# Heads in pairs, a later turning, later constant rows, and a longer lag in the feed-forward stage

## The chip, the core and the metric

The kernel runs on one core of a Trainium2 chip. A core has a matrix engine (TensorE, in the rows PE, with its loads of the stationary operand as PEld), a vector engine (VectorE, DVE), a scalar engine (ScalarE, ACT), a general engine (GpSimd, POOL) and a queue engine (SyncE, SP) that starts transfers. Each engine works through its own list of instructions in order, and waits where an instruction needs what another engine has not yet made. The metric is the device time of one execution in microseconds; less is better.

## The reference: what is computed

Two layers over 256 tokens of width 1024. In each layer a normalised input goes through one wide projection whose columns feed four mixers: A, attention over chunks with a position bias; B, attention on low-rank queries and keys with a rotary part; C, attention with forget sums in the scores; D, a convolution module. A, B and C have four heads of 64 columns each, so there are twelve heads. Each mixer's 256 columns are projected to 1024, multiplied with a sigmoid gate, and summed; an output projection and the residual follow. Then a feed-forward part (FF): `x + square(relu(norm(x) @ w_up)) @ w_down`, with 4096 hidden columns. A last normalisation closes the trunk.

```python
proj = jnp.einsum('bsnc,ncd->bsnd', branches, w_branch)
gates = jax.nn.sigmoid(h @ w_gate + b_gate).reshape(b, s, N_BRANCH, D_MODEL)
x = x + jnp.sum(gates * proj, axis=2) @ w_o
hf = rms_norm(x, g_ffn)
x = x + jnp.square(jax.nn.relu(hf @ w_up)) @ w_down
```

## The kernel before

**Products.** Every product with a weight is made of three matmuls of a reduced float32 format (fp32r): weight and activation are each split into a high part and a remainder, and high x high, high x low and low x high are summed in PSUM (`mm3`, lines 117 to 121). A weight tile (128 x 1024, 512 KB) is loaded by SyncE, its high part is cast by ScalarE (`hi`, L112), and its remainder is subtracted by VectorE (`lo`, L113). There are five buffers for raw tiles and four each for `hi` and `lo`, so a tile is cast when the tile four places ahead of it has been used. The attention itself (scores, transposes, weighted sums) uses plain float32 matmuls, each done in two recorded passes; a transpose is one record.

**Order.** TensorE's order is as written in the program. The order on the other engines is made by the framework's planner, from its own estimate of when each instruction could run.

**Ticks.** Attention is cut into small pieces that are put between the weight products. The list `side` holds 33 slots; each weight tile of a projection or gate ends with `tick()`, which runs the next slot. Slots 0 to 3 fall into the first projections of mixer A, 4 to 7 into `values`, 8 into `mla` (the low-rank projections of B), 9 to 12 into the projections of C, and the rest into `gates`. Head i (0 to 3 of A, 4 to 7 of B, 8 to 11 of C) has its `scores` in slot 4 + 2i, its `transposes` three slots later and its `weighted` sum four slots later. So an even slot holds the weighted sum of head i-2 and the scores of head i, and an odd slot one head's transposes.

**One head.** `scores` (L561) is two products, 128 x 128 and 128 x 256, into one PSUM tile. VectorE adds mask or bias and takes the row extreme (L569), ScalarE takes the exponential with its row sum (L571), VectorE the reciprocal (L573), and GpSimd multiplies (L575, two instructions). Then TensorE transposes three blocks (L581), ScalarE copies them to SBUF (L583), and TensorE makes the weighted sum (L592, L593) into 64 of the 128 rows of a PSUM tile which two heads share: an even head into rows 0 to 63, an odd one into 64 to 127. Mixer A's scores use 64 contraction rows, 0 to 63 for an even head and 64 to 127 for an odd one; those of B and C use all 128. Score tiles come from a pool with one buffer (`psc`), the transposes' from one with two (`pms`), the weighted sums' from one with one (`ppv`).

**Constant rows.** `setup` (L214) makes, once, near the start of layer 0, the one-hot mask `hm` and, with four VectorE instructions (L219), the constant rows of mixer C's query tile `QC`. They are first read by the scores of head 8.

**Branches and output.** Gated branch sums are gathered in `Z[0]` and `Z[1]`, for the two halves of the columns. `turned(c)` transposes half c on TensorE into two PSUM tiles (L759); ScalarE and VectorE split them into `yh` (L761) and `yl` (L762). `output(kp, h)` then multiplies a weight tile of the output projection with blocks 2kp and 2kp+1 of y. Blocks 0 to 3 are half 0, blocks 4 to 7 half 1.

**Feed-forward.** There are 32 tiles. `mtile` makes the first product of tile i (24 matmuls of 256 columns), `hidden(i)` makes relu-squared and splits it (L833 to L836) into a ring of eight, and `second(d, ...)` makes the second product of tile d = i - LAG (12 matmuls of 512 columns, L853 to L857). The first three tiles (`EARLY`) are done ahead of the loop. The last two tiles of the second product (four in the last layer) are held back and done output block by output block after the loop.

Of the kernel before, what the change touches and what calls it, by code (L numbers as in the profile page):

```python
# [17 lines left out]
F32 = mybir.dt.float32  # L18
# [6 lines left out]
P = 128  # L25
# [22 lines left out]
A0 = 4  # L48
CONV_FROM, CONV_TO = 4, 28
WARM = 9  # L50

LAG = 2
RING = 8
FT = 32

# [15 lines left out]
def hybrid_trunk(ctx: ExitStack, tc: tile.TileContext, xT, xtok, pos, small, gfin, bgate, abias, w_lat, w_v, w_in, w_uq, w_ukv,  # L71
# [11 lines left out]
    psc = ctx.enter_context(tc.tile_pool(name="psc", bufs=1, space=bass.MemoryType.PSUM))  # L83
    ppv = ctx.enter_context(tc.tile_pool(name="ppv", bufs=1, space=bass.MemoryType.PSUM))
    pms = ctx.enter_context(tc.tile_pool(name="pms", bufs=2, space=bass.MemoryType.PSUM))
# [4 lines left out]
    def nm(s):  # L90
        count[0] += 1
        return f"{s}_{count[0]}"

    def after(inst, other):
        tc.add_manual_dep(inst.ins, other.ins.name,
                          mybir.DependencyInfo(mybir.DependencyClass.NoSync, mybir.DependencyReason.DATA),
                          reason="order")
# [4 lines left out]
    def weights(src, n=WCOLS, pieces=1, between=None):  # L102
        raw = rawp.tile([P, WCOLS], F32, tag="raw", name=nm("raw"))
        hi = whp.tile([P, WCOLS], F32R, tag="hi", name=nm("hi"))
        lo = wlp.tile([P, WCOLS], F32R, tag="lo", name=nm("lo"))
        w = n // pieces
        for c in range(0, n, w):
            nc.sync.dma_start(raw[:, c:c + w], src[:, c:c + w])
            if c == 0 and between is not None:
                between()  # L110
        for c in range(0, n, w):
            cut = nc.scalar.copy(hi[:, c:c + w], raw[:, c:c + w])  # L112
            done = nc.vector.tensor_tensor(lo[:, c:c + w], raw[:, c:c + w], hi[:, c:c + w], op=ALU.subtract)  # L113
        share[0] = done
        return hi, lo, done, cut
# [98 lines left out]
    def setup(prev):  # L214
        after(nc.gpsimd.tensor_copy(identr, ident), prev)
        after(nc.vector.tensor_reduce(hm, ident.rearrange("p (g c) -> p c g", c=32)[:, 0:HEADS, :], axis=AX, op=ALU.add), share[0])
        for h in range(HEADS):
            f = 64 * (1 - h % 2)
            nc.vector.tensor_scalar(QC[f:f + 32, h, :], tri[f:f + 32, P:T].unsqueeze(1).broadcast_to([32, 2, P]),  # L219
                                    hm[f:f + 32, h:h + 1], None, op0=ALU.mult)  # L220
# [75 lines left out]
    def to_features(half, dst, gcol, pool, tag):  # L296

        for pr in range(2):
            pt = pool.tile([P, 512], F32, tag=tag, name=nm("pt"))
            for j in range(2):  # L300
                k = 4 * half + 2 * pr + j
                for b in range(NB):
                    nc.tensor.transpose(pt[:, j * T + b * P:j * T + (b + 1) * P], X[:, b, k * P:(k + 1) * P], ident)  # L303
            for j in range(2):
                k = 4 * half + 2 * pr + j
                scale_split(dst, k, pt[:, j * T:(j + 1) * T], gcol(k))
# [4 lines left out]
    def ps2(ps):  # L311
        return ps.rearrange("p (a t) -> p a t", a=2)
# [12 lines left out]
    for l in range(L):  # L325
# [5 lines left out]
        side = []  # L331
# [6 lines left out]
        def new_ps(name):  # L338
            return pmm.tile([P, 512], F32, tag="mm", name=nm(name))
# [51 lines left out]
        if l == 0:  # L391
            setup(last_add)
# [143 lines left out]
        def operands(i):  # L536
            mixer, h = divmod(i, HEADS)
            pr, o = h // 2, 64 * (h % 2)
            if mixer == 1:
                return mixer, h, qB[:, h, :], kB[:, h, :], VB, h * HD  # L540
            if mixer == 2:
                return mixer, h, QC[:, h, :], KC[:, h, :], VAC, 256 + h * HD
            return mixer, h, qkA[o:o + 64, pr, :], qkA[o:o + 64, 2 + pr, :], VAC, h * HD
# [10 lines left out]

        def scores(i):
            mixer, h, q, k, _, _ = operands(i)
            S = psc.tile([P, 512], F32, tag="sc", name=nm("S"))
            for b in range(NB):
                sl = S[:, spans[b][0]:spans[b][1]]
                n = (b + 1) * P  # L560
                nc.tensor.matmul(sl, q[:, b * P:(b + 1) * P], k[:, 0:n], start=True, stop=True)  # L561
            mask = (abt[h], maskb, maskc)[mixer]
            mn = tmp.tile([P, NB], F32, tag="mn", name=nm("mn"))
            sme = tmp.tile([P, NB], F32, tag="sme", name=nm("sme"))
            pe = probs[i] = tmp.tile([P, 3 * P], F32, tag="pe", name=nm("pe"))
            for b, (c0, c1) in enumerate(spans):

                bias = mask[:, T - (c1 - c0):T]
                nc.vector.tensor_tensor_reduce(out=pe[:, c0:c1], in0=S[:, c0:c1], in1=bias, scale=-1.0, scalar=-NEG,  # L569
                                               op0=ALU.add, op1=ALU.min, accum_out=mn[:, b:b + 1])  # L570
                last_exp[0] = nc.scalar.activation(pe[:, c0:c1], pe[:, c0:c1], AF.Exp, bias=mn[:, b:b + 1], scale=-1.0,  # L571
                                                   accum_out=sme[:, b:b + 1])
            nc.vector.reciprocal(sme, sme)  # L573
            for b, (c0, c1) in enumerate(spans):
                nc.gpsimd.tensor_scalar(pe[:, c0:c1], pe[:, c0:c1], sme[:, b:b + 1], None, op0=ALU.mult)  # L575
# [95 lines left out]
            tick()  # L671


        NH = 3 * HEADS
        NT = max(A0 + 2 * NH + 3, CONV_TO + 5)
        plan = [[] for _ in range(NT)]
        for i in range(NH):
            plan[A0 + 2 * i].append((2, scores, i))
            plan[A0 + 2 * i + 3].append((1, transposes, i))
            plan[A0 + 2 * i + 4].append((0, weighted, i))  # L680
        side = [[(lambda f=f, i=i: f(i)) for _, f, i in sorted(p, key=lambda e: e[0])] for p in plan]
        side[0].append(position_biases)
        side[0].append(lambda: latents(share[0]))
# [6 lines left out]
        side[4].append(rotary_key_rows)  # L690
        if l == 0:
            side[5].append(rotary_tables)
        side[13].append(forget_sums)
        for t in range(CONV_FROM, CONV_TO):
            n = [2 * CONV_K * (j - CONV_FROM) // (CONV_TO - CONV_FROM) for j in (t, t + 1)]
# [11 lines left out]
        def tokens(ps, st, w, j, first, last):  # L707

            mm3(ps, st, (w[0][:, j * 512:(j + 1) * 512], w[1][:, j * 512:(j + 1) * 512]), first, last, late_mov=True)

        def block(pair, k, b):
            return pair[0][:, k, b * P:(b + 1) * P], pair[1][:, k, b * P:(b + 1) * P]
# [36 lines left out]
        def turned(c):  # L749

            if c == 0:
                y[:] = [act.tile([P, 8, T], F32R, tag="qk1", name=nm("yh")),
                        act.tile([P, 8, T], F32R, tag="qk2", name=nm("yl"))]
            for pr in range(2):
                pt = pms.tile([P, 512], F32, tag="ms", name=nm("pyt"))
                for j in range(2):
                    o = (2 * pr + j) * P
                    for b in range(NB):
                        nc.tensor.transpose(pt[:, j * T + b * P:j * T + (b + 1) * P], Z[c][:, 0, b, o:o + P], ident)  # L759
                ks = slice(4 * c + 2 * pr, 4 * c + 2 * pr + 2)  # L760
                nc.scalar.copy(y[0][:, ks, :], ps2(pt))  # L761
                nc.vector.tensor_tensor(y[1][:, ks, :], ps2(pt), y[0][:, ks, :], op=ALU.subtract)  # L762
# [26 lines left out]
        def joined(b, h):  # L789

            xs = X[:, b, h * 512:(h + 1) * 512]
            nc.vector.tensor_tensor(xs, po[b, h], xs, op=ALU.add)

        def output(kp, h):
            w = weights(w_o[l, kp, h])
            for b in range(NB):
                if kp == 0:
                    po[b, h] = new_ps("po")
                for j in range(2):
                    k = 2 * kp + j  # L800
                    tokens(po[b, h], block(y, k, b), w, j, k == 0, k == KT - 1)
                if kp == 3:
                    joined(b, h)
                    if (h, b) == (1, 0):
                        to_features(0, xg2, gffn, pms, "ms")
# [8 lines left out]
        branch(1, 3)  # L814
        output(0, 1)
        output(1, 0)
        output(1, 1)
        turned(1)
        for kp, h in ((2, 0), (2, 1), (3, 0), (3, 1)):
            output(kp, h)  # L820
        v2 = stream_squares()
# [41 lines left out]
        last = []  # L863
        for i in range(FT + LAG):
            if EARLY <= i < FT:
                ps = new_pu(i)
                mtile(ps[:, :T], w_up[l, i], xg2)
                hidden(i, ps)
            d = i - LAG
            if d < 0:  # L870
# [130 lines left out]
```

## Time and profile before

| what | value |
|---|---|
| time, median of 3 runs | 839.18 us (838.95 to 839.31) |
| time of the profiled execution | 839.31 us |
| its span, first to last instruction | 837.5 us |
| TensorE busy | 818.6 us, 98% |
| VectorE busy | 571.2 us, 68% |
| ScalarE busy | 438.7 us, 52% |
| GpSimd busy | 94.1 us, 11% |
| mean granted TensorE clock | 0.997 |

In a row of the timeline the first number is the start, the second how long the merged instructions lasted; matmuls are pipelined, so they overlap, and the distance between two starts is the time that one takes up. A note in brackets is idle time of the engine ahead of the row, and what ended it. In a row of the waits stand the total, the number of times, and the longest.

### The profile page before, as it was taken

The page shows a single profiled execution, that of the slowest core. Times are in us where ns is not written, and L with a number is a line of the kernel's source. Part 1 is how long each engine was busy: PE and PEld are TensorE (multiplying, and loading weights), DVE is VectorE, ACT ScalarE, POOL GpSimd, SP SyncE. Part 2 cuts the span into 40 slices and gives each one's busy share as a digit, 9 for nine tenths or more (in the row PEclk, how much of TensorE's full clock was granted, in tenths as well). Part 3 has the DMA queues.
Part 4 walks back from the last instruction along what each step waited for, and adds up shares of the span by engine and source line. Part 5 has one row for each costly group of instructions (what it writes and reads, how often), then busy time and mean ns, then how long its engine had stood idle before and what let it go on. Part 6 is the DMA issues. An engine that isn't in the chain of part 4 may idle for free. (4 is left out here: it accounts for less than half of the span.)

```text
span 837.5 us, 12579 instructions
## 1 busy us (share of the span) xinstructions
PE 818.6 (98%) x4718; PEld 708.5 (85%) x4718; DVE 571.2 (68%) x934; ACT 438.7 (52%) x703; POOL 94.1 (11%) x136
## 2 busy tenths in 40 slices
PE   9899999999999999999999999999999999999996
PEld 7888777888789999999899887778887899999994
DVE  7789875689675555555588788658795655555554
ACT  6665656444364444454485664565445544444443
POOL 6212321011100000000000222211120000000000
PEclk9999999999999999999999999999999999999998
DMA  8675545676546666656555545546655666655641
GB/s 273 226 220 165 143 151 165 185 215 200 176 138 191 187 189 190 188 182 196 168 173 177 157 126 170 166 144 200 205 185 176 186 190 183 190 186 186 188 127 51
DMA packets 44973, 148.93 MB, mean 178 GB/s; under 512 B 5488, under 2 KB 7792, under 8 KB 44784
## 3 DMA queue, kind: packets, MB, share of 16 engines
q1 hardware_dynamic: 44336, 146.51, 56.9%
q10 hardware_dynamic: 576, 1.62, 0.6%
q8 instruction: 37, 0.61, 0.3%
q14 instruction: 24, 0.20, 0.1%
HBM read 147.06 MB, written 1.05 MB: 177 GB/s over the span
## 5 line engine op out<-in xcount | busy, mean ns | idle before, releaser
L113 DVE TENSOR_TENSOR lo<-raw,hi 128x1024 fp32r<-128x1024 f32 (+2 forms) x273 | 341.1, 1253 | 199.6 <-ACT hi L112 195.7
L112 ACT CAST hi<-raw 128x1024 fp32r<-128x1024 f32 (+2 forms) x273 | 279.2, 1025 | 338.5 <-issue 213.0
L119 PE MATMUL pu<-xgh,hi 128*128 128x256 f32 x512 | 144.9, 283 | 0.7 <-ACT xgh L293 0.7
L120 PE MATMUL pu<-xgl,hi 128*128 128x256 f32 x512 | 145.1, 283 | 0.3
L121 PE MATMUL pu<-xgh,lo 128*128 128x256 f32 x512 | 144.9, 283 | 0.0
L119 PE MATMUL pgt<-hi,xgh 128*128 128x512 f32 x256 | 105.8, 413 | 0.0
L119 PE MATMUL pd<-hi,u 128*128 128x512 f32 x256 | 100.8, 394 | 1.7 <-ACT u L835 1.7
L120 PE MATMUL pd<-hi,u 128*128 128x512 f32 x256 | 100.7, 393 | 1.0 <-DVE u L836 1.0
L119 PEld LDWEIGHTS pu<-xgh,hi 128*128 128x128 f32 x512 | 98.0, 191 | 3.4 <-ACT xgh L293 1.1
L120 PEld LDWEIGHTS pu<-xgl,hi 128*128 128x128 f32 x512 | 98.0, 191 | 3.0 <-DVE xgl L294 0.7
L121 PE MATMUL pgt<-lo,xgh 128*128 128x512 f32 x256 | 100.1, 391 | 0.0
L120 PE MATMUL pgt<-hi,xgl 128*128 128x512 f32 x256 | 99.9, 390 | 0.0
L121 PE MATMUL pd<-lo,u 128*128 128x512 f32 x256 | 99.6, 389 | 0.0
L121 PEld LDWEIGHTS pu<-xgh,lo 128*128 128x128 f32 x512 | 98.0, 191 | 0.0
L575 POOL TENSOR_SCALAR pe<-pe,sme 128x128 f32<-128x128 f32 (+1 forms) x48 | 45.6, 960 | 171.4 <-DVE sme L573 161.3
L119 PEld LDWEIGHTS pd<-hi,u 128*128 128x128 f32 x256 | 48.3, 189 | 11.0 <-ACT u L835 2.5
L121 PEld LDWEIGHTS pgt<-lo,xgh 128*128 128x128 f32 x256 | 48.1, 188 | 10.8
L121 PEld LDWEIGHTS pd<-lo,u 128*128 128x128 f32 x256 | 48.1, 188 | 10.3
L119 PEld LDWEIGHTS pgt<-hi,xgh 128*128 128x128 f32 x256 | 48.1, 188 | 9.8 <-issue 0.7
L120 PEld LDWEIGHTS pd<-hi,u 128*128 128x128 f32 x256 | 48.3, 189 | 9.5 <-DVE u L836 1.8
L120 PEld LDWEIGHTS pgt<-hi,xgl 128*128 128x128 f32 x256 | 48.2, 188 | 9.3
L491 DVE SCALAR_TENSOR_TENSOR cacc<-up,sm,cacc 128x256 f32<-128x256 f32 x120 | 53.3, 486 | 0.0
(256 smaller groups left out, 1237.7 us busy)
## 6 DMA issues: line engine op xcount, KB each, us to landing
raw<-in_w_gate SPq DMA_DIRECT2D x64, 512.0 KB, 3.7
raw<-in_w_up SPq DMA_DIRECT2D x64, 512.0 KB, 3.8
raw<-in_w_dn SPq DMA_DIRECT2D x64, 512.0 KB, 3.7
raw<-in_w_in SPq DMA_DIRECT2D x23, 512.0 KB, 4.1
raw<-in_w_br SPq DMA_DIRECT2D x16, 512.0 KB, 4.0
raw<-in_w_o SPq DMA_DIRECT2D x16, 512.0 KB, 4.4
raw<-in_w_v SPq DMA_DIRECT2D x8, 512.0 KB, 3.9
bg<-in_bgate SPq DMA_DIRECT2D x16, 256.0 KB, 3.5
```

Source lines behind the costliest of these rows:

```text
L112: cut = nc.scalar.copy(hi[:, c:c + w], raw[:, c:c + w])
L113: done = nc.vector.tensor_tensor(lo[:, c:c + w], raw[:, c:c + w], hi[:, c:c + w], op=ALU.subtract)
L119: nc.tensor.matmul(ps, sh, mh, start=first, stop=False)
L120: nc.tensor.matmul(ps, *((sl, mh) if late_mov else (sh, ml)), start=False, stop=False)
L121: nc.tensor.matmul(ps, *((sh, ml) if late_mov else (sl, mh)), start=False, stop=last)
L491: ins = nc.vector.scalar_tensor_tensor(cacc[:, c, :], up[:, c, j:j + T], wcol, cacc[:, c, :], op0=ALU.mult, op1=ALU.add)
L575: nc.gpsimd.tensor_scalar(pe[:, c0:c1], pe[:, c0:c1], sme[:, b:b + 1], None, op0=ALU.mult)
```

## The change

Heads 2p and 2p+1 now run together: the scores of both stand in slot 4 + 4p, the transposes of both three slots later, the weighted sums of both four slots later. Slots that hold scores or weighted sums are 4, 8, 12, 16, 20, 24 and 28; slots 7, 11, 15, 19, 23 and 27 hold transposes. The score tile of an odd head comes from the pool `pms`. The number of slots stays 33, for the convolution's last step is in slot 32. The four instructions for the constant rows move from `setup` into slot 11 of layer 0. `turned(1)` stands ahead of `output(1, 1)` instead of behind it. LAG is 3 instead of 2, so the loop of the feed-forward stage begins with the first product of tile 3 and then makes the second product of tile 0.

```diff
--- before.py
+++ after.py
@@ -49,7 +49,7 @@
 CONV_FROM, CONV_TO = 4, 28
 WARM = 9
 
-LAG = 2
+LAG = 3
 RING = 8
 FT = 32
 
@@ -214,6 +214,8 @@
     def setup(prev):
         after(nc.gpsimd.tensor_copy(identr, ident), prev)
         after(nc.vector.tensor_reduce(hm, ident.rearrange("p (g c) -> p c g", c=32)[:, 0:HEADS, :], axis=AX, op=ALU.add), share[0])
+
+    def query_ones():
         for h in range(HEADS):
             f = 64 * (1 - h % 2)
             nc.vector.tensor_scalar(QC[f:f + 32, h, :], tri[f:f + 32, P:T].unsqueeze(1).broadcast_to([32, 2, P]),
@@ -554,7 +556,8 @@
 
         def scores(i):
             mixer, h, q, k, _, _ = operands(i)
-            S = psc.tile([P, 512], F32, tag="sc", name=nm("S"))
+            pool, tag = ((psc, "sc"), (pms, "ms"))[i % 2]
+            S = pool.tile([P, 512], F32, tag=tag, name=nm("S"))
             for b in range(NB):
                 sl = S[:, spans[b][0]:spans[b][1]]
                 n = (b + 1) * P
@@ -671,13 +674,15 @@
             tick()
 
 
+
         NH = 3 * HEADS
-        NT = max(A0 + 2 * NH + 3, CONV_TO + 5)
+        NT = max(A0 + 2 * NH + 1, CONV_TO + 5)
         plan = [[] for _ in range(NT)]
         for i in range(NH):
-            plan[A0 + 2 * i].append((2, scores, i))
-            plan[A0 + 2 * i + 3].append((1, transposes, i))
-            plan[A0 + 2 * i + 4].append((0, weighted, i))
+            t = A0 + 4 * (i // 2)
+            plan[t].append((2, scores, i))
+            plan[t + 3].append((1, transposes, i))
+            plan[t + 4].append((0, weighted, i))
         side = [[(lambda f=f, i=i: f(i)) for _, f, i in sorted(p, key=lambda e: e[0])] for p in plan]
         side[0].append(position_biases)
         side[0].append(lambda: latents(share[0]))
@@ -690,6 +695,7 @@
         side[4].append(rotary_key_rows)
         if l == 0:
             side[5].append(rotary_tables)
+            side[11].append(query_ones)
         side[13].append(forget_sums)
         for t in range(CONV_FROM, CONV_TO):
             n = [2 * CONV_K * (j - CONV_FROM) // (CONV_TO - CONV_FROM) for j in (t, t + 1)]
@@ -814,8 +820,8 @@
         branch(1, 3)
         output(0, 1)
         output(1, 0)
+        turned(1)
         output(1, 1)
-        turned(1)
         for kp, h in ((2, 0), (2, 1), (3, 0), (3, 1)):
             output(kp, h)
         v2 = stream_squares()
```

## Rows read from the trace of the kernel before

**Rows 1.** Page: busy time of the engines; 40 slices of VectorE and of the clock.

```profile
PE 818.6 (98%) x4718; PEld 708.5 (85%) x4718; DVE 571.2 (68%) x934; ACT 438.7 (52%) x703; POOL 94.1 (11%) x136
...
DVE  7789875689675555555588788658795655555554
...
PEclk9999999999999999999999999999999999999998
```

**Rows 2.** Waits of TensorE over the whole span: us in total, times, longest us.

```profile
PE pqk L121 <- DVE lo L113: 2.0, 2, 1.5
PE po L120 <- DVE yl L762: 1.7, 2, 0.9
PE pd L119 <- ACT u L835: 1.7, 3, 1.1
...
PE pg L121 <- DVE lo L113: 1.0, 1, 1.0
```

**Rows 3.** Timeline of TensorE (start us, us, instructions): an even tick, mixer B.

```profile
89.07 0.39 PE L121 MATMUL pgt<-lo,xgh 128*128 128x512 f32 x1
...
91.18 0.39 PE L120 MATMUL pgt<-hi,xgl 128*128 128x512 f32 x1
91.41 0.39 PE L121 MATMUL pgt<-lo,xgh 128*128 128x512 f32 x1
```

**Rows 4.** Timeline of TensorE: a tick with scores alone, mixer A.

```profile
56.69 0.39 PE L121 MATMUL pv<-lo,xgh 128*128 128x512 f32 x1
...
58.19 0.39 PE L120 MATMUL pv<-hi,xgl 128*128 128x512 f32 x1
```

**Rows 5.** Timeline of TensorE: a tick with weighted sum and scores, mixer A.

```profile
73.14 0.28 PE L121 MATMUL pqk<-xgh,lo 128*128 128x256 f32 x1
...
75.22 0.28 PE L120 MATMUL pqk<-xgl,hi 128*128 128x256 f32 x1
```

**Rows 6.** Timeline of TensorE: a tick with a weighted sum alone.

```profile
148.79 0.39 PE L121 MATMUL pgt<-lo,xgh 128*128 128x512 f32 x1
...
150.24 0.40 PE L120 MATMUL pgt<-hi,xgl 128*128 128x512 f32 x1
```

**Rows 7.** Timeline of TensorE: the forget sums, plain float32 passes.

```profile
85.89 0.60 PE L471 MATMUL pf<-tri,lfc 128*128 128x256 f32 x2
86.32 0.38 PE L472 MATMUL pf<-tri,lfc 128*128 128x128 f32 x2
```

**Rows 8.** Timeline of TensorE: turning of half 0, then of half 1.

```profile
200.03 1.03 PE L759 MATMUL pyt<-ident,Z 128*128 128x128 f32 x8
...
201.13 0.40 PE L120 MATMUL pbr<-hi,brl 128*128 128x512 f32 x1
...
222.68 1.04 PE L759 MATMUL pyt<-ident,Z 128*128 128x128 f32 x8
...
225.60 0.50 PE L120 MATMUL po<-hi,yl 128*128 128x512 f32 x1 [0.87 <-DVE yl L762]
```

**Rows 9.** Timeline of VectorE: the last sums into half 1 of Z.

```profile
216.62 1.30 DVE L745 TENSOR_TENSOR Z<-Z 128x512 f32<-128x512 f32 x2 [1.10 <-POOL Z L747]
```

**Rows 10.** Timeline of TensorE: from the early first FF products to the second.

```profile
247.68 0.28 PE L121 MATMUL pu<-xgh,lo 128*128 128x256 f32 x1
...
249.54 0.40 PE L121 MATMUL pd<-lo,u 128*128 128x512 f32 x1
```

**Rows 11.** Timeline of VectorE and GpSimd near the start of the kernel.

```profile
18.95 2.63 DVE L219 TENSOR_SCALAR QC<-tri,hm 32x256 f32<-32x256 f32 x4
...
21.52 1.21 DVE L113 TENSOR_TENSOR lo<-raw,hi 128x1024 fp32r<-128x1024 f32 x1
...
19.99 0.74 POOL L385 TENSOR_TENSOR acc<-acc 128x256 f32<-128x256 f32 x1
```

**Rows 12.** Timeline of TensorE and GpSimd: one head of mixer B, scores to transposes.

```profile
82.04 0.92 PE L561 MATMUL S<-qkB 128*128 128x128 f32 x4
...
86.00 2.68 POOL L575 TENSOR_SCALAR pe<-pe,sme 128x128 f32<-128x128 f32 x2 [6.76 <-DVE sme L573]
...
93.70 0.49 PE L581 MATMUL pT<-ident,pe 128*128 128x128 f32 x3
```

## Prediction

> **What bounds the kernel now.** I read the page first. TensorE is busy for 818.6 of the 837.5 us span, and its clock row is 9 throughout (the 8 is the last slice), so the full clock of 2.4 GHz is granted nearly everywhere; VectorE stands at 68% [rows 1]. So TensorE's own list is the path, and only two things shorten it: waits inside it, and time in which it is counted busy without streaming columns. The second view is the list of TensorE's waits. They are short and few; of those that the change can touch, the output product waits for `yl`, the second FF product for `u`, and an early projection for `lo` [rows 2]. For the third I read the timeline by starts: matmuls overlap in it, so the distance between two starts is what one costs. 512 columns in fp32r cost 0.23 us (91.18 to 91.41) [rows 3], 256 half of that. Whatever a small attention step adds to this beat is its cost. It shows what the busy share hides: each step costs more than its passes.
>
> **Heads in pairs.** I take the distance from the last projection matmul before a step to the second one after it, less two matmuls. A weighted sum with scores of B costs 91.18 - 89.07 - 0.46 = 1.65 us [rows 3]. Scores alone (A) cost 58.19 - 56.69 - 0.46 = 1.04 [rows 4]. A weighted sum with scores of A, among 256-column matmuls, costs 75.22 - 73.14 - 0.24 = 1.84 [rows 5]. A weighted sum alone costs 150.24 - 148.79 - 0.46 = 0.99 [rows 6]. The passes themselves are cheaper: two plain float32 passes of 256 columns take 86.32 - 85.89 = 0.43 us [rows 7], so 0.216 each and, as my estimate, 0.108 for 128 columns. Scores are two of each, as is a weighted sum: 0.65 us. So a step of scores and sum carries 1.65 - 1.30 = 0.35 us of seams, one sum alone 0.34, scores of A alone 0.39, and the mixed step of A 0.54.
>
> Before, a layer has in slots 4 to 30: scores of A alone twice, the mixed step of A twice, the mixed step of B or C eight times, a sum alone twice. Seams: 0.78 + 1.08 + 2.80 + 0.68 = 5.34 us. After, the passes are the same, but there are seven such steps: scores of A once (0.39), the step of A once (0.54), of B or C four times (1.40), sums alone once (0.34). That is 2.67. The saving is 2.67 us a layer, 5.3 for both, if a second head behind a first of the same kind costs its bare passes.
>
> That condition is what the trace does not show: no two sums, and no two scores of A, stand next to each other there. There are 16 new joints: 6 sums and 2 scores of A a layer, each with the two heads in different halves of the array. From above, a joint costs what an ordinary seam does, 0.34 / 2 = 0.17 us [rows 6, 7], 2.7 us in all. From below, passes of different halves overlap, and a joint gains one pass of 128 columns, 0.108, 1.7 us in all. I take zero, by the nearest row: the two passes of the forget sums, each with its own load of the stationary operand, follow one another at the bare 0.216 [rows 7]. The part is worth 5.3 us, between 2.6 and 7.0. Transposes in pairs gain nothing that counts, since they show no seam worth naming.
>
> The Trainium skill speaks against a free joint ("TensorE: Matmul & The Clock Gate", Part 3, What overlaps and what doesn't): a stationary load overlaps running matmuls only if its row group differs. By it the twelve joints of sums, which use the same rows and other columns, would each show their load, and only the four of A would be hidden; [rows 7], where loads into the same rows are hidden, contradict it as it stands.
>
> What the pairs move on other engines: two heads' reductions, exponentials and products come at once, and the transposes are three slots later as before. For a head of B, scores start at 82.04, GpSimd's two products run from 86.00 to 88.68, and the transposes start at 93.70 [rows 12]: 11.66 us in all, 6.64 used. In the new order the interval loses a transposes step (3 x 0.108 = 0.32) and a mixed step (1.65) and gains one head's scores (0.65): 10.34 us. The second head's products queue behind the first's, another 2.68 at this row's rate: 9.32. That leaves 1.0 us, so I price it at zero; if that cover is gone, each late pair costs what it is late. The odd score tile takes a `pms` buffer, but VectorE has emptied it before the transposes three slots on ask for two.
>
> **The turning.** Turning half 1 and restarting takes 225.60 - 222.68 = 2.92 us; turning half 0, followed by other work, takes 201.13 - 200.03 = 1.10 [rows 8]. The difference, 1.82 us a layer, is the wait for `yh` and `yl`. Afterwards `output(1, 1)` stands behind it, 12 x 0.23 = 2.8 us of matmuls [rows 3], more than the 1.82. The turning then starts 2.8 us earlier, at 219.9, and its last input, the sum into `Z`, is done at 216.62 + 1.30 = 217.92 [rows 9]: 2.0 us to spare. Bounds: nothing to 1.82 a layer; a loss is excluded, because the wait could only change its place. I take all of it: 3.6 us.
>
> **The lag.** From the last early first product to the third matmul of the second product takes 249.54 - 247.68 = 1.86 us [rows 10] against 0.12 + 2 x 0.23 = 0.58 unhindered. So 1.28 us a layer is the wait for tile 0's `u`, and `mtile(3)` (24 x 0.12 = 2.9 us) now covers it. Its weight tile takes the place in the load order that tile 0 of the second product had, and that one made nobody wait: in [rows 2] the second product waits for `u` alone. Gain 2.6 us for two layers, between 0 and 2.6. The 1.1 us wait of the same row is the last layer's end; it hangs on the last tile's `u` and stays, since the order of the last four tiles does.
>
> **The constant rows.** The four instructions hold VectorE from 18.95 to 21.52, behind GpSimd's sums until 19.99 + 0.74 = 20.73 [rows 11]. Behind them waits the remainder for which TensorE stands 1.0 us [rows 2]. Without them it can start at 20.73 at the latest (I let it wait for GpSimd, because beside GpSimd's sums even these four small instructions took 2.63 us): 21.52 - 20.73 = 0.8 us gained. The normalisation factor, on which the later early waits hang, stands behind the same remainder and moves with it, so they do not eat the gain. In slot 11 the four cost VectorE up to 2.6 us where it is at 9 tenths (fourth slice) [rows 1]; the cover there is the 1.0 us left to a pair of B [rows 12]. So the part lies between 1.0 - 2.6 = -1.6 and the whole wait, +1.0. I take +0.8.
>
> **Sum.** 5.3 + 3.6 + 2.6 + 0.8 = 12.3 us from the profiled execution's 839.31 (837.5 of span and 1.8 around it): 827.0. The median of the runs shown is 0.13 lower, so 826.9.
>
> **Rivals.** (1) No joint is free. For it: every change of shape in [rows 3 to 6] shows a seam. Against: [rows 7]. Sixteen joints at 0.17 cost 2.7 us: 829.6. Chance 0.12.
> (2) Only the joints of sums cost, since two sums use the same 128 contraction rows and other columns, while A's scores use other rows: twelve at 0.17, 2.0 us: 828.9. Chance 0.08, for [rows 7] stand against it. This is the Trainium skill's rule from above, put as a mechanism of this kernel.
> (3) Some pairs are late: in layer 0, where VectorE is fullest and now has the constant rows, or where the planner puts weight remainders ahead of a reduction. Three pairs late by 1 us, and the constant rows gaining nothing: 826.9 + 3.0 + 0.8 = 830.7. For it: 1.0 us of room. Against: GpSimd's 2.68 is a slow pair of products. Chance 0.12.
> (4) Slower: the second head's last product lands more than 2.0 us later than reckoned, at all twelve pairs, since two heads' reductions now queue behind two remainders (1.21 us each, second row of [rows 11]). It eats the 1.0 us of room and then 1.03 us at each transposes step, 12.3 us in all; from there on the kernel is slower: 840 to 842. Against: no wait before transposes is long enough to stand among the terms of [rows 2], and 9.32 is already reckoned with a slow pair of products. Chance 0.07, with 0.02 of it where it stops within 0.2%.
> (5) The moves do not do what they say: the planner delays `Z`, or `lo` of tile 3, and the waits only change place: 826.9 + 3.6 + 2.6 = 833.1. Chance 0.04.
>
> **How the numbers follow.** The forecast has 0.57, the rivals 0.12, 0.08, 0.12, 0.07 and 0.04. The range reaches down to overlapping joints and the upper bound of the constant rows (826.9 - 1.7 - 0.2 = 825.0) and up past rivals 1 to 3, to 831.5; rivals 4 and 5 are left out. About 0.2% (1.7 us) is what a measurement can tell from no change: faster 0.93 (the forecast and rivals 1, 2, 3 and 5), within 0.02 and slower 0.05 (both from rival 4).
>
> **What would show it.** In the profile after: seven steps with scores or sums a layer, the one of B or C at 1.65 + 1.30 = 2.95 us; no wait of the output product for `yl`; no wait of the second FF product for `u` but the last; the early wait for `lo` under 0.3 us; no wait of TensorE before transposes. A mixed step of 3.1 us is rival 1 or 2. A wait of the transposes for GpSimd is rival 3 or 4. The prediction is wrong if other waits of more than 4 us in all stand in TensorE's list, or if the pairs' steps do not shrink.

## The result, and the profile after

The changed kernel takes 816.26 us (median of 4 runs, 815.97 to 816.69) against 839.07 for the kernel before: a ratio of 0.9728, 95% interval 0.9711 to 0.9745. The forecast was 826.9 us, range 825.0 to 831.5. The direction was right; the gain is 22.8 us instead of 12.3, and the time lies well below the range.

The page first: busy times, then the slices of VectorE and of the clock, as in [rows 1].

```profile
PE 799.2 (98%) x4718; PEld 701.9 (86%) x4718; DVE 571.2 (70%) x934; ACT 438.2 (54%) x703; POOL 96.8 (12%) x136
...
DVE  7799885789675555555588889667886655555554
...
PEclk9999999999999999999999999999999999999999
```

TensorE executes the same 4718 records as before and is busy 19.4 us less. Neither fewer instructions nor a faster clock does that; the same matmuls occupy the engine for less time. Next the waits of TensorE (total, times, longest), against [rows 2].

```profile
PE pqk L121 <- DVE lo L113: 2.0, 2, 1.5
...
PE pg L121 <- DVE lo L113: 1.0, 1, 1.0
PE pd L119 <- ACT u L841: 1.0, 1, 1.0
```

The output product no longer waits for `yl` or `yh`, and the second FF product waits for `u` once instead of three times. The early wait of `pg` for `lo` is still there, at 1.0 us. Now the starts on TensorE. From the first scores to the first branch product, from there to the first FF product, and from there to the next layer (in layer 1, to the last matmul), the stretches took:

| stretch | layer 0 before | after | layer 1 before | after |
|---|---|---|---|---|
| attention and gates | 117.55 | 109.34 | 117.07 | 108.88 |
| branches, turning, output | 69.91 | 67.99 | 69.92 | 67.99 |
| feed-forward | 183.89 | 182.56 | 184.39 | 182.98 |

That is 16.4, 3.9 and 2.7 us for the two layers; another 0.4 us lies ahead of the first scores. Together they are, to rounding, the 23.3 us by which the span of the profiled execution shrank (837.5 to 814.2).

Most of it is in attention, so there the single steps have to be read. First the mixed step of mixer B, which answers to [rows 3], on TensorE (start, length, instructions):

```profile
92.59 0.39 PE L121 MATMUL pgt<-lo,xgh 128*128 128x512 f32 x1
92.90 0.66 PE L595 MATMUL pPV<-pts,VB 128*64 128x256 f32 x4
93.39 0.39 PE L596 MATMUL pPV<-pts,VB 128*64 128x128 f32 x4
93.71 1.58 PE L564 MATMUL S<-qkB 128*128 128x128 f32 x8
94.94 0.58 PE L119 MATMUL pgt<-hi,xgh 128*128 128x512 f32 x1
95.36 0.40 PE L120 MATMUL pgt<-hi,xgl 128*128 128x512 f32 x1
```

It costs 95.36 - 92.59 - 0.46 = 2.31 us for two heads, where 2.95 was forecast and 1.65 was the price of one head before. The second row is the one that counts: from the start of its four passes of 256 columns (x4, two heads) to the start of the next row, 92.90 to 93.39, it is 0.49 us; one behind the other, four passes would take 4 x 0.216 = 0.86. The step with sums alone, which answers to [rows 6], shows the same:

```profile
134.27 0.39 PE L121 MATMUL pgt<-lo,xgh 128*128 128x512 f32 x1
134.58 0.66 PE L595 MATMUL pPV<-pts,VAC 128*64 128x256 f32 x4
135.07 0.40 PE L596 MATMUL pPV<-pts,VAC 128*64 128x128 f32 x4
...
135.73 0.40 PE L120 MATMUL pgt<-hi,xgl 128*128 128x512 f32 x1
```

Two heads' sums cost 135.73 - 134.27 - 0.46 = 1.00 us; before, one head's cost 0.99 [rows 6]. The second head is free. Through a window that ends 10 ns after the start of this step, one of the four passes has begun; through one that ends 20 ns after it, two have:

```profile
134.58 0.44 PE L595 MATMUL pPV<-pts,VAC 128*64 128x256 f32 x2
```

They last 0.44 us together. Two such passes of one head last 0.65 (the run with heads of the same half, below), so these two belong to different heads.

The scores of mixer A do the same. In slot 4 the scores of both heads take 50.32 - 49.46 = 0.86 us up to the transposes of the rotary key:

```profile
49.46 0.93 PE L564 MATMUL S<-qkA 64*128 64x128 f32 x8
50.32 0.44 PE L451 MATMUL pkr<-ident,kr 128*128 128x128 f32 x2
```

Two heads of B, whose scores use all 128 rows, take 94.94 - 93.71 = 1.23 us by their starts, as two times the passes would.

The turning and the lag, for [rows 8] and [rows 10]:

```profile
211.38 1.04 PE L765 MATMUL pyt<-ident,Z 128*128 128x128 f32 x8
...
212.48 0.39 PE L120 MATMUL po<-hi,yl 128*128 128x512 f32 x1
```

```profile
240.05 0.28 PE L121 MATMUL pu<-xgh,lo 128*128 128x256 f32 x1
240.17 0.40 PE L119 MATMUL pd<-hi,u 128*128 128x512 f32 x1
240.41 0.40 PE L120 MATMUL pd<-hi,u 128*128 128x512 f32 x1
240.64 0.39 PE L121 MATMUL pd<-lo,u 128*128 128x512 f32 x1
```

Turning half 1 and going on takes 1.10 us, as half 0 did; the first second-product runs at the beat, 240.64 - 240.05 = 0.59.

The constant rows, for [rows 11], on VectorE:

```profile
18.29 2.98 DVE L221 TENSOR_SCALAR QC<-tri,hm 32x256 f32<-32x256 f32 x4
21.19 1.21 DVE L113 TENSOR_TENSOR lo<-raw,hi 128x1024 fp32r<-128x1024 f32 x1
```

They were written into slot 11 of the program and did not move on the engine: still at 18 us, still ahead of the remainder for which TensorE waits.

Last the way of a pair of mixer B from scores to transposes, for [rows 12]:

```profile
79.12 1.58 PE L564 MATMUL S<-qkB 128*128 128x128 f32 x8
...
83.58 4.43 POOL L578 TENSOR_SCALAR pe<-pe,sme 128x128 f32<-128x128 f32 x4 [9.74 <-DVE sme L576]
...
89.42 0.82 PE L584 MATMUL pT<-ident,pe 128*128 128x128 f32 x6
```

From scores to transposes it is 10.30 us (10.34 reckoned), and GpSimd's four products end at 88.01, 1.4 us before they are needed.

### The profile page after: what moved, and what is told of

Its sections match the earlier page's. It is cut to its first block, busy times and chain, and to the rows that moved or that the text cites. A ratio compares the mean times of both kernels' runs of the same rounds, so it can differ in the third digit from the quotient of the medians.

```text
span 814.2 us, 12587 instructions
## 1 busy us (share of the span) xinstructions
PE 799.2 (98%) x4718; PEld 701.9 (86%) x4718; DVE 571.2 (70%) x934; ACT 438.2 (54%) x703; POOL 96.8 (12%) x136
## 4 chain that ended last, share of the span: by engine, by line
PE 93%; DVE 2%; issue 1%; ACT 1%; DMA 1%; POOL 1%; SPq 0%; POOLq 0%; DVEq 0%; ACTq 0%
PE pu L120 7%; PE pu L121 7%; PE pu L119 7%; PE pgt L119 7%; PE pgt L121 7%; PE pgt L120 7%; PE pd L119 7%; PE pd L120 7%; PE pd L121 7%; PE S L564 2%; PE pqk L121 2%; PE po L121 2%; PE po L119 2%; PE pbr L121 2%; PE po L120 2%; PE pqk L119 2%
## 5 line engine op out<-in xcount | busy, mean ns | idle before, releaser
L119 PE MATMUL pgt<-hi,xgh 128*128 128x512 f32 x256 | 103.1, 403 | 0.0
L578 POOL TENSOR_SCALAR pe<-pe,sme 128x128 f32<-128x128 f32 (+1 forms) x48 | 48.3, 1022 | 139.5 <-DVE sme L576 115.3
L121 PEld LDWEIGHTS pd<-lo,u 128*128 128x128 f32 x256 | 48.1, 188 | 10.4
```

Of the source, the lines that this page charges most:

```text
L119: nc.tensor.matmul(ps, sh, mh, start=first, stop=False)
L121: nc.tensor.matmul(ps, *((sh, ml) if late_mov else (sl, mh)), start=False, stop=last)
```

## The experiments

Theory A: two heads whose sums lie in different halves of the array's columns, or whose scores lie in different halves of its rows, run side by side, so that the second costs next to nothing. Rival B: what was saved is seams, in more places than were reckoned, or it comes from the other edits.

**Pairs alone.** Only the plan and the second pool of score tiles, on the kernel before.

```diff
+            pool, tag = ((psc, "sc"), (pms, "ms"))[i % 2]
...
+            t = A0 + 4 * (i // 2)
+            plan[t].append((2, scores, i))
+            plan[t + 3].append((1, transposes, i))
+            plan[t + 4].append((0, weighted, i))
...
```

> Only the pairs, on the kernel before; turning, lag and constant rows as before. Theory A (two heads whose sums or scores lie in different halves of the array run side by side, so the second costs next to nothing): the attention stretches shrink by 8.2 us a layer as in the changed kernel, 839.1 - 16.4 = 822.7 us. Rival B (the pairs bring only the saved seams, 2.67 us a layer, and the rest comes from the other edits): 833.8 us.

822.6 us (822.41 to 822.9), 0.9805 of before (0.979 to 0.9819). The pairs bring 16.3 us by themselves, so the excess is theirs.

**Heads of the same half.** Pairs are heads 0 and 2, then 1 and 3, and the sums of all four heads of a mixer go into one PSUM tile, in two halves of its columns.

```diff
-            t = A0 + 4 * (i // 2)
+            m, h = divmod(i, HEADS)
+            t = A0 + 8 * m + 4 * (h % 2)
...
-            if h % 2 == 0:
+            if h == 0:
...
-            po = pvt[mixer]
+            po = pvt[mixer][:, pr * T:(pr + 1) * T]
```

> The changed kernel, but pairs are heads 0 and 2, then 1 and 3: both sums of a pair then lie in the same 64 columns of the array, and both scores of mixer A in the same 64 rows; number, shape and slots of all steps unchanged. Theory A (side by side in different halves): 12 sums and 4 scores of A cost their 0.65 us again, +10.4, so 826.7 us, and a weighted sum alone of two heads takes 1.65 us above the beat instead of 1.01. Rival B (fewer seams, wherever the heads lie): 816.3 us, no change.

841.56 us, a miss for both theories. The kernel had a wait of its own making, shown in the list of TensorE's waits:

```profile
PE pPV L595 <- DVE brl L600: 10.6, 6, 1.8
```

The sum of head 3 waited for the copy of what head 1 had just put into the same tile. These waits make up 10.6 of the 15.2 us between this run and the clean one below; in the profiled execution the clock was also lower for a while after three of them (last section). With both copies behind head 3's sum the test is clean:

```diff
-            if h % 2 == 1:
-                j = 2 * mixer + pr
+            if h == 3:
+                for j in (2 * mixer, 2 * mixer + 1):
```

> As the run with pairs 0 and 2, 1 and 3, but both copies of a mixer's sums stand behind its last sum, since there the sum of head 3 waited 1.8 us for the copy of the tile half that head 1 had just filled. Theory A (side by side in different halves): 826.7 us, that is +10.4 on the changed kernel, 0.65 us for each of 12 sums and 4 scores of A, and no wait of sums. Rival B (fewer seams wherever the heads lie): 816.3 us.

826.37 us (826.01 to 826.56), 10.1 above the changed kernel, where A says 10.4 and B nothing. Its step with sums alone, on TensorE:

```profile
138.83 0.39 PE L121 MATMUL pgt<-lo,xgh 128*128 128x512 f32 x1
139.15 0.65 PE L595 MATMUL pPV<-pts,VAC 128*64 128x256 f32 x2
139.63 0.38 PE L596 MATMUL pPV<-pts,VAC 128*64 128x128 f32 x2
139.85 0.59 PE L595 MATMUL pPV<-pts,VAC 128*64 128x256 f32 x2
140.28 0.38 PE L596 MATMUL pPV<-pts,VAC 128*64 128x128 f32 x2
...
140.93 0.40 PE L120 MATMUL pgt<-hi,xgl 128*128 128x512 f32 x1
```

Where there was one row x4 there are two rows x2, one after the other, and the step costs 140.93 - 138.83 - 0.46 = 1.64 us instead of 1.00. The scores of A, now in the same rows, take 1.50 us by their starts instead of 0.86:

```profile
49.51 1.57 PE L564 MATMUL S<-qkA 64*128 64x128 f32 x8
51.01 0.44 PE L451 MATMUL pkr<-ident,kr 128*128 128x128 f32 x2
```

The number of steps and their shapes are those of the changed kernel, so the difference is the halves alone. B falls. For the sums, the half of the array's columns and the half of the PSUM rows are one choice in the program, and no run parts the two; for the scores of A only the rows of the array change.

These rows settle the disputed joint too. From 139.63 to 139.85 two passes of 128 columns take 0.22 us, the bare rate: a second sum in the same half costs its bare passes and no seam, which is what the prediction assumed for all joints.

**Neighbours or not.** The pairs of the changed kernel, in the order sum, scores, sum, scores.

```diff
-        side = [[... sorted(p, key=lambda e: e[0])] for p in plan]
+        side = [[... sorted(p, key=lambda e: (e[2] % 2, e[0]))] for p in plan]
```

> The changed kernel, but in the five slots a layer that hold sums and scores of a pair the order is sum, scores, sum, scores instead of sum, sum, scores, scores; heads, halves, slots and all other engines' work unchanged. Theory A (side by side only while the two stand next to each other): each of the ten slots loses the overlap of its sums (0.65 us), the two slots with scores of A that of the scores as well (0.65), and each gains two seams (0.34): 6.5 + 1.3 + 3.4, +11.2 us, 827.5 us. Rival E (TensorE finds the other half free past a product that stands between): the two seams alone, +3.4, 819.7 us.

827.23 us (827.09 to 827.75), 11.0 above the changed kernel, as A says. In the mixed step each head's sum is x2 again:

```profile
96.17 0.65 PE L595 MATMUL pPV<-pts,VB 128*64 128x256 f32 x2
96.65 0.38 PE L596 MATMUL pPV<-pts,VB 128*64 128x128 f32 x2
96.96 0.92 PE L564 MATMUL S<-qkB 128*128 128x128 f32 x4
97.81 0.65 PE L595 MATMUL pPV<-pts,VB 128*64 128x256 f32 x2
98.30 0.38 PE L596 MATMUL pPV<-pts,VB 128*64 128x128 f32 x2
98.61 0.92 PE L564 MATMUL S<-qkB 128*128 128x128 f32 x4
```

TensorE did not reach past the scores that stand between the two sums, and E falls: to run side by side, the two heads had to be neighbours.

**Turning back, lag back.** Each undone in the changed kernel.

```diff
-        turned(1)
         output(1, 1)
+        turned(1)
```

> The changed kernel with the turning of half 1 behind output(1, 1) again. If the two waits for yh and yl come back as they were: +3.7 to +3.9 us, 820.1 us. If the shorter attention stage has left VectorE and ScalarE freer there: less than +2 us.

820.21 us (819.75 to 820.31): +3.9. Both waits are back as they were (`po` for `yl` 1.7 us, for `yh` 1.0 us, twice each).

```diff
-LAG = 3
+LAG = 2
```

> The changed kernel with LAG 2. If the wait for u of tile 0 comes back twice: +2.6 us, 818.9 us. If the lag also helped the end of the last layer: up to +3.5 us.

818.76 us (818.71 to 819.45): +2.5. The wait for `u` is back at 1.7 us in three places; the longest of them, the last layer's end, is 1.1 us against 1.0 in the changed kernel.

**Constant rows.** First written in `setup` again, as before the change; then tied behind the last weight remainder.

```diff
-            nc.vector.tensor_scalar(QC[f:f + 32, h, :], ...)
+            after(nc.vector.tensor_scalar(QC[f:f + 32, h, :], ...), share[0])
```

> The changed kernel with the four constant-row instructions written in setup again. Theory C (the planner places them by when they could run, so writing them into slot 11 moved nothing on VectorE): 816.3 us within 0.3. Rival D (they did move in effect and the 0.3 us gained in the first 50 us is theirs): 816.6 to 817.1 us.

> The changed kernel with the four constant-row instructions tied behind the last weight remainder ahead of slot 11, so that VectorE does run them there. If the price in the prediction holds: 0.8 us less, 815.5 us, the early wait for lo (1.0 us) nearly gone. If a later early wait takes it back: 816.3 us. If VectorE is too full at slot 11: up to 817.9 us.

Written early: 815.96 us (815.72 to 816.43), not to be told from the changed kernel. The four run at 19.11 us, behind `hm` and ahead of the remainder, as they do in the changed kernel, so their new place in the program was no move at all. Nor is the 0.4 us ahead of the first scores theirs: those start at 49.83 us before, 49.46 in the changed kernel and 49.95 here, so this stretch differs as much between two executions with the same order. Tied: 815.45 us (815.22 to 815.6), 0.5 below the run beside it and 0.8 below the changed kernel. VectorE then turns to the remainder 2.6 us earlier:

```profile
18.07 0.17 DVE L216 TENSOR_REDUCE hm<-ident 128x4 f32<-128x16 f32 x1
18.64 1.75 DVE L113 TENSOR_TENSOR lo<-raw,hi 128x1024 fp32r<-128x1024 f32 x1 [0.40 <-ACT hi L112]
```

The four instructions run between 64.6 and 67.4 us, 1.4 us instead of 2.9, and nobody waits for them. Of the 1.0 us wait that goes, a part comes back just ahead, where the wait for the sums of squares (`pc` for `acc`) grows from 0.2 to 0.5 us. So the size forecast for this edit, 0.8, came out at 0.5 to 0.8 for an edit that was not in the change.

**A version that beats both.** As the last, and in the last layer three tiles of both halves of block 0 are multiplied ahead of the last tile.

```diff
+            if b == 0:
+                for h in range(2):
+                    for d, w in last[:-1]:
+                        second(d, w, b, h)
...
-                    for d, w in last:
+                    for d, w in last if b else last[-1:]:
```

> As const_held, and in the last layer the first three held-back tiles of both halves of token block 0 are done ahead of the last tile, so that 2.0 us more of matmuls cover the last tile's u. The wait of 1.0 us before it and the slow start behind it (1.5 us in all) should go: 1.3 to 1.5 us below const_held, 814.0 us. If the end hangs on something else: as const_held.

814.41 us (813.99 to 814.56), 0.9706 of before (0.9693 to 0.9719), 1.0 below the run with the rows tied. The wait for the last tile's `u` is gone from the list. From the first scores to the last matmul its profiled execution is 1.5 us shorter than that with the rows tied (755.71 against 757.26), as expected, and ahead of the first scores it is 0.2 us longer; why the medians differ by 1.0 and not by 1.3 was not followed further.

## Why the prediction was right or wrong

| term | forecast | measured | by |
|---|---|---|---|
| heads in pairs | 5.3 | 16.3 | pairs alone |
| turning | 3.6 | 3.9 | undone |
| lag | 2.6 | 2.5 | undone |
| constant rows | 0.8 | 0 | written early: no difference |
| sum | 12.3 | 22.7 | all together: 22.8 |

**The step that failed is the price of the joint, taken as zero and at best as a gain of one short pass**, in the part on the pairs: "From below, passes of different halves overlap, and a joint gains one pass of 128 columns, 0.108". I had seen that the two heads lie in different halves of the array, and let only the last pass of one overlap the first of the other, as if the engine started matmuls strictly one behind the other. In the trace the whole second head runs beside the first. A joint gains not 0.108 but the 0.64 us of all four passes (1.00 against 1.64 us). Twelve sums and four scores of A make 16 x 0.64 = 10.2 us. With that in place of the zero the pairs would have been priced at 15.5, the sum at 22.5, and the time at 816.7. That this is within 0.5 us of the 816.26 measured is luck in part: the 0.8 us of the constant rows in it did not come, and the pairs brought 16.3, 0.8 more than 15.5. For these the prediction had no term. Its distance ends at the second matmul behind a step, and the next six are still slow: in the trace of the kernel before, six distances behind a step, from 124.21 to 125.60 us, make 1.39 us, and six far from one, in the trace after, from 127.02 to 128.38, make 1.36. Between the first scores and the first branch product small steps stand among the weight products 29 times before and 18 times after (layer 0); added up over the starts of these matmuls it is 0.4 us a layer.

The value I took, a second head at its bare passes, was right for heads in the same half. The seams were right as well: the mixed step of B carries 2.31 - 3 x 0.65 = 0.36 us of them (bare passes of 0.65 us for two heads' scores and for one sum, as the other sum runs beside it), and the run with the order split, which adds two seams a slot, came out 0.3 us from the sum worked out from [rows 3 to 6]. So rivals 1 and 2, dear joints, were not only wrong but wrong in sign.

The Trainium skill's sentence that I weighed (Part 3 of "TensorE: Matmul & The Clock Gate") made me look for a hidden load, when the same part says something larger: small matmuls at different tile positions of the array run concurrently. The Trainium skill gives a distance of about 4 ns between their starts; here it is between 10 and 20 ns, and the saving is the whole second head. By itself that sentence would not have given the right term. Were matmuls started strictly in the order of the program, as the Trainium skill says too (cited in the last section), only the last pass of the first head, 128 columns, could run beside the first pass of the second, and that is my lower bound again. What I lacked is shown by the rows alone: the second head's first pass starts 10 to 20 ns behind that of the first head, ahead of all its other passes.

**The constant rows** failed at "Without them it can start at 20.73". The remainder was not without them: the planner, which orders VectorE by when an instruction could run, put them where they had been. Rival 5 named such a case, but for other edits. In the front part it is said who orders VectorE; I did not ask it of this edit. That the rows, once tied, gave 0.5 to 0.8 us is no support for the working either: the remainder then started at 18.64 us, 2.6 us earlier and not 0.8, and the wait for the sums of squares took back part of the 1.0 us.

**What held.** The turning and the lag, to 0.3 and 0.1 us, each from one distance between starts with and without the wait. Nothing was late behind the pairs: no wait of the transposes stands in TensorE's list, and for the first pair of B GpSimd was done 1.4 us ahead, where 1.0 was reckoned, so rivals 3 and 4 had no ground. The last layer's wait for `u` stayed, as said.

## What to carry to other kernels

Ask of every pair of neighbouring small matmuls which rows and columns of the array they use; if they share none and are alike in size, as the heads are here, price the second at nothing, and order the program so that such matmuls stand next to each other. Fewer and larger steps between the weight products save a seam of 0.34 to 0.54 us each in this kernel, but only neighbours in different halves save the work itself. Where a planner orders an engine, moving a line in the program moves nothing by itself: look up in the trace whether the instruction moved, and tie it if it must.

## What the runs showed of the hardware

The two products of a sum stand in the program as 256 columns, then 128, head after head. In the trace all four 256-column passes (L595 x4) start before any 128-column pass (L596). So a second head's first product started ahead of the first head's second one, and the front part's sentence that each engine works through its list in order does not hold for them. The Trainium skill ("TensorE: Matmul & The Clock Gate", Part 2, Step-by-step) says that matmuls stay in program order; for products in different halves of the columns these rows show otherwise.

In the run with heads of the same half and the extra wait, three of the six waits were followed by a lower clock. These are stretches of its trace: length, busy time by engine, and after those the granted clock (PEclk). The first three lie around the first wait, the next two behind two others, and the last behind one that left the clock alone.

```profile
82.00:84.00 2.00, 0.93 (x5) 0.61 (x6) 1.96 (x4) 0.03 (x1) 0.00 (x0) 0.99 0.37 152
84.00:86.00 2.00, 2.00 (x7) 1.81 (x8) 0.99 (x5) 0.43 (x2) 0.00 (x0) 0.50 0.36 86
86.00:88.00 2.00, 2.00 (x7) 1.56 (x6) 1.36 (x9) 1.71 (x8) 0.00 (x0) 0.65 0.44 176
...
150.00:152.00 2.00, 2.00 (x6) 1.51 (x6) 0.00 (x0) 0.00 (x0) 0.00 (x0) 0.50 0.18 72
...
560.00:562.00 2.00, 2.00 (x6) 1.53 (x5) 0.00 (x0) 0.00 (x0) 0.00 (x0) 0.54 0.08 31
...
495.00:497.00 2.00, 2.00 (x13) 1.75 (x12) 1.63 (x9) 0.91 (x4) 0.00 (x0) 1.00 0.36 53
```

TensorE had stood 1.78 us up to 83.07, and then ran at 0.50, the lower level of 1.2 GHz, until some way into the third stretch; the scores there took 2.85 us instead of 1.58. The waits that ended at 147.48 and 557.04 us were followed by the same level. The other three left the clock at 1.00, though all six are between 1.75 and 1.78 us long, and the one that ended at 494.26 is the same wait in layer 1 as the first. What decides it is open here.
